# Nearest-neighbour upsampling: another order of the loads, and a first store of 56 rows

## The chip, the cores and the metric

The kernel runs on one core of one Trainium2 chip. The metric is device time of that core in microseconds (us), the median of several runs; lower is better. Beside the runs there is one profiled execution, from which all views of the trace come; its times count from the first instruction of the program.

## The reference

```python
def reference(x, scale_factor):                 # x: 16 x 64 x 64 x 64 float32, scale_factor 2
    ...
    for i in range(new_h):
        for j in range(new_w):
            src_i = i // scale_factor
            src_j = j // scale_factor
            result[:, :, i, j] = x[:, :, src_i, src_j].copy()
    return result.astype(np.float32)
```

Every input element becomes a block of 2 x 2 output elements. 16.78 MB come in, 67.11 MB go out, and nothing is calculated.

## The kernel before

**Tiling.** The input is a list of 65536 rows of 64 floats. It is cut into four quarters (`Q = 4`); in each quarter a partition holds 128 consecutive rows (`RQ`), so that all four quarters give a partition 512 rows. One input row of 64 floats becomes 256 output floats (two equal rows of 128), that is 1 KB of output a row.

**Memory.** One tile `mem` fills most of the on-chip memory: 79 output rows of free room (`WF`), and behind it the whole input (`xt`, 512 rows of 64 floats), the quarters in their natural order whatever the order of the loads.

**Loads (line 153).** Four DMAs, one for each quarter, issued by SyncE on its one queue. `begin_before_barrier` moves these four issues ahead of the opening barrier of the program.

**Groups (lines 162 to 177).** The 512 rows are worked off in order in ten groups, whose row counts stand in `rows` (line 141). For each group the rows are expanded within the on-chip memory (source: 64 floats a row, each read twice, the whole row twice; destination: one contiguous run), and then one DMA stores the group. Group 0 is copied by VectorE alone (line 171). Of the others VectorE copies `k * 9 // 32 * 2` rows, an even number, and ScalarE the rest (line 173). The store (line 176) is issued by SyncE on the same queue as the loads.

**Where the expanded rows lie.** Even groups start at offset 0 of `mem`, in the free room. Odd groups end just in front of the first input row that is not expanded yet, over input rows that are already used up. So group n + 2 takes room of group n and has to wait until store n has landed, and the copy of group n + 2 runs while store n + 1 is on the wire. Group 1 overwrites the input rows of group 0, so that its copies wait for the copy of group 0.

**Order.** All DMAs stand on one queue and are served in the order of their issue. SyncE waits before each store for the copies of its group. The waits follow from the overlaps in `mem`: a copy waits for the load of its input rows.

**End.** `close_early` rearranges the closing barrier so that only the wait for the last store stands at the end. The change does not touch it.

Of the kernel before, what the change touches and what calls it, by code (L numbers as in the profile page):

```python
# [1 line left out]

# [4 lines left out]

EARLY = 4  # L10


def begin_before_barrier(nc):

    blocks = nc.main_func.blocks
    main, body = blocks[0], blocks[1]
    sp = mybir.EngineType.SP
    loads = [i for i in body.instructions if i.engine == sp][:EARLY]  # L20
    for load in loads:
        assert isinstance(load, mybir.InstDMACopy), type(load)
        assert not (load.sync_info and load.sync_info.on_wait)
    names = [i.name for i in loads]
    body.instructions = [i for i in body.instructions if i.name not in names]
    kept = list(main.instructions)
    at = next(
        n
        for n, i in enumerate(kept)
        if i.engine == sp and isinstance(i, mybir.InstDrain)  # L30
    )
    kept[at:at] = loads
    main.instructions = kept


def close_early(nc):

    blocks = nc.main_func.blocks  # L40
    sp, pool = mybir.EngineType.SP, mybir.EngineType.Pool
    stores = [
        i
        for i in blocks[1].instructions
        if i.engine == sp and isinstance(i, mybir.InstDMACopy)
    ]
    last = stores[-1].sync_info.on_update[0].id

    end = list(blocks[-1].instructions)
    wait = end[0]  # L50
    assert wait.engine == sp and isinstance(wait, mybir.InstDrain)
    waits = list(wait.sync_info.on_wait)
    assert len({w.id for w in waits}) == len(waits) > 2
    assert all(w.wait_mode == "sem-ge-imm" for w in waits)

    mine = [i for i in end if i.engine == pool]
    kinds = [type(i).__name__ for i in mine]
    assert kinds == [
        "InstDrain",
        "InstEventSemaphore",  # L60
        "InstEventSemaphore",
        "InstDrain",
        "InstISA",
        "InstDrain",
        "InstEventSemaphore",
        "InstEventSemaphore",
    ], kinds
    d0, gather0, release0, d1, clear, d2, gather1, release1 = mine


    lo, hi = clear.ant_dict["range_first"], clear.ant_dict["range_last"]
    assert lo <= last <= hi and all(lo <= w.id <= hi for w in waits)
    clears = []
    for a, b in ((lo, last), (last + 1, hi + 1)):
        if a < b:
            clears.append(nc.gpsimd.sem_clear(range(a, b)).ins)

    landed = mybir.InstDrain(
        name=wait.name,
        engine=pool,  # L80
        debug=wait.debug,
        sync_info=mybir.SyncInfo(
            on_wait=[w for w in waits if w.id != last], on_update=[]
        ),
    )
    (w,) = [w for w in waits if w.id == last]
    final = mybir.InstEventSemaphore(
        name=clear.name,
        engine=sp,
        debug=wait.debug,  # L90
        sync_info=mybir.SyncInfo(
            on_wait=[w],
            on_update=[
                mybir.SyncUpdate(
                    sync_type=w.sync_type,
                    id=w.id,
                    ant_name=w.ant_name,
                    update_mode="sem-sub-imm",
                    update_value=w.wait_value,
                )  # L100
            ],
        ),
    )
    others = [i for i in end if i.engine != pool and i is not wait]
    blocks[-1].instructions = others + [
        d0, gather0, release0, gather1, release1, d1, landed, *clears, d2, final
    ]


@with_exitstack  # L110
def kernel(
    ctx: ExitStack,
    tc: tile.TileContext,
    x: bass.AP,
    scale_factor: int,
    out: bass.AP,
):
    nc = tc.nc
    nc.at_finalize(begin_before_barrier)
    nc.at_finalize(close_early)  # L120
    P = nc.NUM_PARTITIONS
    s = int(scale_factor)
    B, C, H, W = x.shape
    R = B * C * H // P
    fdt = x.dtype

    Q = 4
    RQ = R // Q  # L130
    xp = x.rearrange("b c h w -> (b c h) w").rearrange(
        "(q p r) w -> q p r w", q=Q, p=P
    )
    op = out.rearrange("b c (h hd) w -> (b c h) (hd w)", hd=s).rearrange(
        "(q p r) w -> q p r w", q=Q, p=P
    )

    rows = [63, 31, 34, 44, 42, 42, 64, 64, 64, 64]
    GROW = s * s
    FREE = 79
    WF = FREE * GROW * W
    assert sum(rows) == R
    mem_pool = ctx.enter_context(tc.tile_pool(name="mem", bufs=1))
    mem = mem_pool.tile([P, WF + R * W], fdt, name="mem")
    xt = mem[:, WF:].rearrange("p (r w) -> p r w", r=R)

    for q in range(Q):
        nc.sync.dma_start(out=xt[:, q * RQ : (q + 1) * RQ], in_=xp[q])

    def expanded(r0, r1):
        return (
            xt[:, r0:r1].unsqueeze(2).unsqueeze(4).to_broadcast([P, r1 - r0, s, W, s])
        )

    r0 = 0  # L160
    before = (0, 0)
    for n, k in enumerate(rows):
        size = k * GROW * W
        at = 0 if n % 2 == 0 else WF + r0 * W - size
        assert at >= before[1] or at + size <= before[0]
        before = (at, at + size)
        u = mem[:, at : at + size].rearrange(
            "p (k a w b) -> p k a w b", k=k, a=s, w=W
        )
        kv = k if n == 0 else k * 9 // 32 * 2  # L170
        nc.vector.tensor_copy(out=u[:, :kv], in_=expanded(r0, r0 + kv))  # L171
        if kv < k:
            nc.scalar.copy(out=u[:, kv:], in_=expanded(r0 + kv, r0 + k))  # L173
        q, f = divmod(r0, RQ)
        assert f + k <= RQ
        nc.sync.dma_start(out=op[q, :, f : f + k, :], in_=u)  # L176
        r0 += k


# [1 line left out]
_INS = ['x', 'scale_factor']  # L181
_OUTS = [((16, 64, 128, 128), 'float32')]

_NUMBERS = {'scale_factor': 2}


# [26 lines left out]
```

## Time and profile before

| | us |
|---|---|
| median of 3 runs (lowest, highest) | 198.25 (198.16, 198.26) |
| the profiled execution | 198.35 |
| its span, first to last instruction | 197.0 |
| VectorE busy, 10 copies | 51.2 |
| ScalarE busy, 9 copies and one table load | 46.3 |

Some words on reading the lines. DVE is VectorE, ACT is ScalarE, SP is SyncE, and a "q" behind a name means its sequencer. L171 is line 171. A group of instructions has its form (partitions x elements), its count, the busy time, the mean time of one in ns, and the idle time of its engine before it with what ended it. A timeline row has start and length in us. A row of windows has the stretch, its width, the busy time of DVE, ACT and POOL with counts, the granted clock, the DMA share and GB/s; share and GB/s count each packet whole in the window in which it starts, so that a narrow window can show more than 1.00. A DMA issue row has KB and the time from issue to landing.

### The profile page before, as it was taken

The numbers are of one execution on the slowest core, as the hardware profiler recorded it, in microseconds if no ns is written. First come the engines' busy times: TensorE is split into PE (matmuls) and PEld (weight loads), VectorE is DVE, ScalarE is ACT, GpSimd is POOL, SyncE is SP. The second block draws the span as 40 slices with busy tenths as digits, with TensorE's granted clock in tenths as the row PEclk, the third lists the DMA queues.
The fourth block names the chain that finished last, engine by engine and source line by source line (L and its number), as shares of the span: only waits on it lengthen the run. The fifth ranks groups of instructions, "written<-read, shape, count | busy, mean of one in ns | idle before, by whom it ended". The sixth has DMA issues, their size and how long they took to land.

```text
span 197.0 us, 107 instructions
## 1 busy us (share of the span) xinstructions
DVE 51.2 (26%) x10; ACT 46.3 (24%) x10; POOL 0.2 (0%) x4
## 2 busy tenths in 40 slices
DVE  0059993000005060510602706300720081000000
ACT  0020006000005262592002906500797000000000
POOL 0000000000000000000000000000000000000000
DMA  8999999999997999999999999999999999999994
GB/s 319 426 426 426 432 432 432 406 512 432 419 419 335 470 422 403 511 421 400 472 437 428 419 419 426 426 426 426 426 466 452 466 492 452 426 426 439 426 426 213
DMA packets 2016, 83.89 MB, mean 426 GB/s; under 512 B 224, under 2 KB 224, under 8 KB 224
## 3 DMA queue, kind: packets, MB, share of 16 engines
q1 hardware_dynamic: 2016, 83.89, 99.2%
HBM read 16.78 MB, written 67.11 MB: 426 GB/s over the span
## 4 chain that ended last, share of the span: by engine, by line
DMA 63%; DVE 13%; ACT 7%; issue 0%; DVEq 0%; ACTq 0%; SPq 0%
DMA out_dram<-mem 57%; DVE mem L171 13%; ACT mem L173 7%; DMA mem<-in_x_dram 6%; DVEq L171 0%; ACTq L173 0%; SPq L176 0%
## 5 line engine op out<-in xcount | busy, mean ns | idle before, releaser
L171 DVE COPY mem<-mem 128x9216 f32<-128x9216 f32 (+5 forms) x10 | 51.2, 5119 | 112.3 <-DMA out_dram<-mem 100.1
L173 ACT COPY mem<-mem 128x7168 f32<-128x7168 f32 (+3 forms) x9 | 45.0, 5005 | 92.9 <-DMA out_dram<-mem 77.2
L173 ACT ACT_TABLE_LOAD x1 | 1.3, 1283 | 12.2 <-DMA mem<-in_x_dram 12.2
L194 POOL MEMSET const-bfloat16-1.0<- 128x1 bf16 x1 | 0.1, 101 | 0.0
L194 POOL MEMSET const-uint8-127<- 128x1 uint8 x1 | 0.1, 101 | 0.0
L194 POOL MEMSET const-float32-0.0<- 128x1 f32 x1 | 0.1, 98 | 0.2 <-issue 0.2
L194 POOL MEMSET const-float32-1.0<- 128x1 f32 x1 | 0.1, 98 | 0.0
## 6 DMA issues: line engine op xcount, KB each, us to landing
mem<-in_x_dram SPq DMA_DIRECT2D x4, 4096.0 KB, 26.0
out_dram<-mem SPq DMA_DIRECT2D x2, 5376.0 KB, 21.8
out_dram<-mem SPq DMA_DIRECT2D x1, 8064.0 KB, 32.3
out_dram<-mem SPq DMA_DIRECT2D x1, 5632.0 KB, 19.0
out_dram<-mem SPq DMA_DIRECT2D x1, 4352.0 KB, 16.0
out_dram<-mem SPq DMA_DIRECT2D x1, 3968.0 KB, 38.2
out_dram<-mem SPq DMA_DIRECT2D x4, 32.4
```

The lines of the kernel that those rows point to most:

```text
L171: nc.vector.tensor_copy(out=u[:, :kv], in_=expanded(r0, r0 + kv))
L173: nc.scalar.copy(out=u[:, kv:], in_=expanded(r0 + kv, r0 + k))
L194: nc = _bacc.Bacc("TRN2", target_bir_lowering=False, num_devices=1)
```

## The change

The loads are issued in the order second, third, first, fourth quarter. They still go to the same places in `xt`, and the groups are still worked off from the first quarter on, so that group 0 now reads what the third load brings. The row counts of the first six groups change; each three still add up to 128. Group 0 is still copied by VectorE alone.

```diff
-    rows = [63, 31, 34, 44, 42, 42, 64, 64, 64, 64]
+    rows = [56, 36, 36, 48, 40, 40, 64, 64, 64, 64]
...
-    for q in range(Q):
+    for q in (1, 2, 0, 3):
         nc.sync.dma_start(out=xt[:, q * RQ : (q + 1) * RQ], in_=xp[q])
```

## The prediction

> **What bounds the kernel now.** I read the page first, then the waits, then short windows around the one place where the DMA queue turns from loads to stores.
>
> ```profile
> span 197.0 us, 107 instructions
> DVE 51.2 (26%) x10; ACT 46.3 (24%) x10; POOL 0.2 (0%) x4
> q1 hardware_dynamic: 2016, 83.89, 99.2%
> HBM read 16.78 MB, written 67.11 MB: 426 GB/s over the span
> ```
>
> The two copying engines work a quarter of the time each. The one DMA queue is occupied for 99.2% of 16 engines' span. So the kernel lasts as long as 83.89 MB take to move, and only what lies between transfers, or slows them, can be won or lost.
>
> ```profile
> DVE mem L171 <- DMA out_dram<-mem: 100.1, 8, 30.0
> ACT mem L173 <- DMA out_dram<-mem: 77.2, 6, 28.9
> 70.00:196.00 126.00, 29.38 (x7) 38.04 (x7) 0.00 (x0) 1.00 1.00 433
> ```
>
> The first two rows (waits) say that from the third copy on, the copying engines wait for stores to land and free their buffer, not the stores for them. The third row is a window: busy time of DVE, ACT and POOL, granted clock, DMA share, GB/s. From 70 to 196 us the queue has a share of 1.00 and moves 433 GB/s. Nothing is to be had there.
>
> The queue is served in order: load 1 to 4, then store 1, 2 and so on. A window as wide as the spread of the 16 engines holds one packet of each, so that share times width is the mean time of a packet: a window of 1.00 us shows it directly. A load packet is 32 KB (16 of them in 1.00 us show as 524 GB/s).
>
> ```profile
> 36.50:37.50 1.00, 0.00 (x0) 0.00 (x0) 0.00 (x0) 1.00 1.21 524
> 37.70:38.70 1.00, 0.00 (x0) 0.00 (x0) 0.00 (x0) 1.00 1.51 524
> 39.30:40.30 1.00, 0.00 (x0) 0.00 (x0) 0.00 (x0) 1.00 1.87 524
> 41.37:42.02 0.65, 0.00 (x0) 0.00 (x0) 0.00 (x0) 1.00 3.68 1588
> 43.70:44.70 1.00, 0.00 (x0) 0.00 (x0) 0.00 (x0) 1.00 2.38 1032
> ```
>
> A load packet takes 1.21 us, but the last two of load 4 on each engine take 1.51 and 1.87: 0.30 + 0.66 = 0.96 us lost on every engine. The fourth row is the first packet of store 1: 16 packets start between 41.37 and 42.02 and take 3.68 x 0.65 = 2.39 us, no more than the second (2.38). So the turn from reading to writing costs 0.96 us, and it is booked on the tail of the loads, not on the head of the stores.
>
> ```profile
> 0.89 0.43 SPq L153 DMA_DIRECT2D mem<-in_x_dram  x1
> mem<-in_x_dram SPq DMA_DIRECT2D x1, 4096.0 KB, 30.6
> 29.14 0.35 SPq L176 DMA_DIRECT2D out_dram<-mem  x1
> ```
>
> The third load is issued at 0.89 and lands 30.6 later, at 31.5. Store 1 is issued at 29.14, so it has been queued for over 8 us when those two slow packets begin. My reading: once an engine has read the last of load 4 it goes straight on to reading store 1 out of SBUF, while the end of load 4 is still being written into SBUF, and the two share a path.
>
> **The change, part by part.** *Order of the loads.* Four DMAs of 4096 KB on one queue, in another order: same bytes, same four issues ahead of everything else. The first quarter is now the third to land, so the first copy may not start before 31.5. The second and third quarter, which are first used by the fourth and seventh copy, land earlier than before; the fourth is last as before. Cost by itself: nothing.
>
> *First copy.* 56 rows of 256 output elements, 14336, on VectorE alone.
>
> ```profile
> 12.16 16.95 DVE L171 COPY mem<-mem 128x16128 f32<-128x16128 f32 x1 [12.16 <-DMA mem<-in_x_dram]
> 29.14 2.29 DVE L171 COPY mem<-mem 128x4096 f32<-128x4096 f32 x1
> L171 DVE COPY mem<-mem 128x4096 f32<-128x4096 f32 x1 | 2.3, 2294 | 0.0
> L171 DVE COPY mem<-mem 128x5632 f32<-128x5632 f32 x2 | 6.2, 3094 | 17.1 <-DMA out_dram<-mem 17.1
> L171 DVE COPY mem<-mem 128x9216 f32<-128x9216 f32 x4 | 19.8, 4960 | 46.0 <-DMA out_dram<-mem 46.0
> ```
>
> Two rates stand here. The copies of 4096 to 9216 elements lie on one line: (4960 - 2294) / 5120 = 0.521 ns an element and 161 ns fixed (5632 gives 3.094, measured 3.094). The first, of 16128, took 1.051 ns an element, twice as much. It differs in size, and in that its 63 rows are odd; every other VectorE part has an even row count by the code (16, 18, 24, 22, 22, 36). Transfers are not the reason: the 4096 one ran at the fast rate at 29.14, with loads still in flight. 14336 at the fast rate is 0.16 + 7.47 = 7.63 us, at the slow rate 15.07. By size it is nearer to the slow row; I take the fast one, since the fast rows show no bend up to 9216 and 56 is even. The Trainium skill ("VectorE: DVE Perf Modes", Mode 2×_2P) says that a one-source copy within SBUF gets two elements a cycle when the outermost dimension is even in source and destination, or odd and equal in both. Here the destination is one contiguous run and the source has 63 rows outermost, so by it 63 is slow and 56 fast; the trace agrees on all ten copies.
>
> So the first copy runs from 31.5 to 39.15 and store 1 is issued at 39.18 (before: the copy ended at 12.16 + 16.95 = 29.11, the issue came at 29.14). That is 10 us later than before, and the question is whether the queue notices.
>
> ```profile
> 0.00 1.89 SPq L153 DMA_DIRECT2D mem<-in_x_dram  x4
> 0.95:1.95 1.00, 0.00 (x0) 0.00 (x0) 0.00 (x0) 1.00 1.82 524
> 2.80:3.33 0.53, 0.00 (x0) 0.00 (x0) 0.00 (x0) 1.00 2.29 989
> 30.63:31.16 0.53, 0.53 (x1) 0.53 (x1) 0.00 (x0) 1.00 2.31 989
> ```
>
> *Would load 4 be over?* Its first packets start between 30.63 and 31.16 (last row: 2.31 x 0.53 = 1.21 us each). With no store behind it all eight would take 1.21, and it would end at 30.63 + 8 x 1.21 = 40.3 on the first engine and 40.85 on the last. So store 1 is issued 1.1 to 1.7 us before the engines run out.
>
> *How long from issue to stream?* The trace shows one start of an idle queue, load 1, issued at 0.00. All 16 first packets start 0.95 to 1.95 us after the issue and take 1.82 instead of 1.21; the second ones start at 2.80 to 3.33, which is as if a steady stream had begun 1.59 (first engine) to 2.12 us (last) after the issue. For store 1 that gives 39.18 + 1.59 = 40.77 to 39.18 + 2.12 = 41.30. Before, its packets began at 41.37 to 42.02. The stream of stores starts 0.60 to 0.72 us earlier, taken as 0.66: the 0.96 lost on the tail is saved, and some 0.3 us of it is given back in engines that wait for the late store. Bounds: at best the whole 0.96 is saved (store data come at once). At worst within this reading, the last first packet starts 1.95 after the issue and carries the full 0.61 extra: 39.18 + 1.95 + 0.61 = 41.74, a gain of 0.28. I keep 0.66, since it is the measured case of an idle queue.
>
> *The other row counts.* Bytes and number of stores stay the same, and the packet rate does not depend on their size (433 GB/s in the long window over all sizes). The pairs must still cover each other: copy n+2 runs while store n+1 is on the wire. The smallest store of the middle is now 36 rows, 4.7 MB, 10.9 us at 433 GB/s.
>
> ```profile
> L173 ACT COPY mem<-mem 128x7168 f32<-128x7168 f32 x4 | 24.7, 6167 | 36.8 <-DMA out_dram<-mem 36.7
> L173 ACT COPY mem<-mem 128x5120 f32<-128x5120 f32 x3 | 13.4, 4459 | 11.6 <-DMA out_dram<-mem 11.6
> L173 ACT COPY mem<-mem 128x4096 f32<-128x4096 f32 x1 | 3.6, 3607 | 28.9 <-DMA out_dram<-mem 28.9
> L173 ACT ACT_TABLE_LOAD x1 | 1.3, 1283 | 12.2 <-DMA mem<-in_x_dram 12.2
> ```
>
> ScalarE's part ends last. Of 36 rows it copies 16 (4096 elements, 3.61 us), of 48 it copies 22 (5632, about 4.9 between the rows for 5120 and 7168), of 64 it copies 28 (6.17). Add 2.1 to restart a queue: 7.0 against the 10.9 of a 36-row store, 8.3 against the 12.1 of a 40-row one. All hidden, with 3.8 us to spare at least; were that gone, each boundary would cost what is missing. Store 2 is issued at 39.18 + 3.61 = 42.8, behind 16.9 us of store 1 (7.34 MB at 433 GB/s). ScalarE's table load waits for the same load as before, now at 31.5; it ends 6 us before ScalarE's first copy. On SyncE nothing but the later stores is queued behind the longer wait.
>
> *Sum.* The profiled execution took 198.35 with its span of 197.0; less 0.66 is 197.69. The median of the runs is 198.25, 0.10 below, so 197.6.
>
> **The rivals.** *The turn is paid anyway.* The 0.96 could belong to the change of direction itself and not to the store queued behind the loads. For it: the trace has only this one turn. Against it: it sits on load packets, and the first store packet shows nothing. If the tail stays slow whatever is queued, the late store hides under it and nothing changes, 198.25; if it is paid after the restart, the last engine starts at 41.30 + 0.96 = 42.26 against 42.02, 198.5. Both are within what can be told from no change: I take 0.2%, 0.4 us, for that, throughout.
>
> *The queue runs dry (slower).* Place: between load 4 and store 1. No row shows a store put into an empty queue. It has to fetch from SBUF with nothing read ahead and then write to HBM; if that costs the turn and one more start of 0.61 us (1.82 - 1.21, seen for a load), the last engine starts at 41.30 + 0.96 + 0.61 = 42.87, 0.85 later than now: 199.1; half of the second part gives 198.8. It becomes a loss once issue to stream exceeds 42.02 - 39.18 = 2.84 us, and a loss of 0.4 at 3.24. Against it: the measured 2.12, and the first store packet of 2.39. The Trainium skill ("DMA: Bandwidth & Descriptors", Rules for kernel authors) speaks against this change: it advises to issue a DMA early, so that its fixed cost overlaps, and under Anatomy of one DMA puts that cost at about 2.0 us, for a DMA issued from GpSimd. By that figure, as an estimate, store 1 would begin at 39.18 + 2.0 = 41.2, hardly before today's first packet, and the gain would be 0.2 us; no row here shows which part of it falls ahead of the data.
>
> *The first copy is slow because it is large.* At 1.051 ns an element it takes 15.07, ends at 46.6, and the stream starts at 46.6 + 2.12 = 48.7, 6.7 us late: 205.0. It decides from a copy of 8.3 us on (7.63 + 0.72). For it: the one copy above 9216 elements is the slow one. Against it: the straight line of the others and the row counts.
>
> **How the numbers follow.** Chances: forecast 0.58, turn paid anyway 0.22, dry queue 0.15, slow copy 0.05. A little of the forecast (its worst bound, 198.0) counts as no change, 0.03, and some 0.01 of the dry queue does: faster 0.55, same 0.26, slower 0.19. Time 197.6. The range goes from 197.2 (0.96 saved is 197.3, and 0.1 for the spread of the runs) to 198.9, which takes in the turn and over half of the dry queue; the slow copy and the rest stay out. The forecast alone would have 197.2 to 198.0.
>
> **What would show it.** Load 4 now:
>
> ```profile
> 1.36 0.53 SPq L153 DMA_DIRECT2D mem<-in_x_dram  x1
> mem<-in_x_dram SPq DMA_DIRECT2D x1, 4096.0 KB, 41.0
> ```
>
> In the profile after: the first VectorE copy starts at 31.5 and takes 7.6 us; store 1 is issued near 39.2; the last two rounds of load 4 take close to 1.21 us, and load 4 lands over half a microsecond earlier than 1.36 + 41.0 = 42.4; the first packets of store 1 take longer than the second ones and the second ones start about 0.66 earlier than a shift by size alone would have it; a share of 1.00 from there to the end, and a span of 196.3. The prediction is wrong if the tail is as slow as before with the store not yet queued, if the first packets of store 1 end later than they did relative to their size, or if the copy takes 15 us.

## The result and the profile after

| | before | after |
|---|---|---|
| median of 21 runs, us | 198.26 | 197.93 |
| lowest to highest | 198.05 to 198.60 | 197.81 to 198.23 |
| span of the profiled execution | 197.0 | 196.7 |

The ratio of the two is 0.9983, with a 95% interval of 0.9976 to 0.9990: 0.33 us less, clear of zero, and half of the forecast 0.66. By the bound of 0.4 us that the prediction set, this counts as no change. The time lies within the range given, 197.2 to 198.9. The span is 196.7 where 196.3 was expected.

The page after, its lines on span, engines and queue:

```profile
span 196.7 us, 108 instructions
DVE 42.8 (22%) x10; ACT 46.1 (23%) x10; POOL 0.2 (0%) x4
q1 hardware_dynamic: 2016, 83.89, 99.1%
```

VectorE is busy 8.4 us less (the first copy runs at the fast rate now), and none of that shows in the time. A round, in what follows, is one packet on each of the 16 engines. Shown are the timeline of VectorE and SyncE, the two rows of load 4 (issue, then KB and time to landing), and windows of the kernel after: the second load round, the last load round, the first two store rounds and the last one. The last row is the last store round of the kernel before:

```profile
31.68 7.63 DVE L171 COPY mem<-mem 128x14336 f32<-128x14336 f32 x1 [31.68 <-DMA mem<-in_x_dram]
39.34 0.35 SPq L176 DMA_DIRECT2D out_dram<-mem  x1
1.36 0.53 SPq L153 DMA_DIRECT2D mem<-in_x_dram  x1
mem<-in_x_dram SPq DMA_DIRECT2D x1, 4096.0 KB, 40.0
...
2.99:3.43 0.44, 0.00 (x0) 0.00 (x0) 0.00 (x0) 1.00 2.76 1192
39.29:39.73 0.44, 0.44 (x2) 0.38 (x1) 0.00 (x0) 1.00 2.76 1192
40.59:41.09 0.50, 0.50 (x1) 0.50 (x1) 0.00 (x0) 1.00 4.32 1835
42.74:43.24 0.50, 0.00 (x0) 0.21 (x1) 0.00 (x0) 1.00 4.28 1835
193.32:193.87 0.55, 0.00 (x0) 0.00 (x0) 0.00 (x0) 1.00 4.40 1907
...
193.59:194.24 0.65, 0.00 (x0) 0.00 (x0) 0.00 (x0) 1.00 3.72 1613
```

Share times width is again the mean packet. The last round of load 4 takes 2.76 x 0.44 = 1.21 us: the slow tail is gone, and load 4 lands at 1.36 + 40.0 = 41.4 instead of 42.4. Now follow the engine that is last in each round, by the right edge of its window; it need not be the same engine in every round. From the second load packet to the first store packet it took 42.02 - 3.33 = 38.69 before. After the change load 4 ends at 39.73 + 1.21 = 40.94, which is 37.51 after 3.43: 1.18 saved. The first store packet then starts at 41.09, 0.15 later. From the first store packet to the last one it took 194.24 - 42.02 = 152.22 before, and 193.87 - 41.09 = 152.78 after: 0.56 lost, spread over 153 us in which the queue does not run empty (a share of 1.00 from 120 to 190 us). With 0.10 by which this execution began its stream later (3.43 against 3.33), the sum is -1.18 + 0.15 + 0.56 + 0.10 = -0.37, and the last packets start 0.37 earlier.

So the change won more than was thought at the turn, and gave 0.7 of it back, most of it in a place where nothing had been expected: the stores themselves run 0.4% slower to the end.

### The profile page after: what moved, and what is told of

Its sections match the earlier page's. It is cut to its first block, busy times and chain, and to the rows that moved or that the text cites. A ratio compares the mean times of both kernels' runs of the same rounds, so it can differ in the third digit from the quotient of the medians.

```text
span 196.7 us, 108 instructions
## 1 busy us (share of the span) xinstructions
DVE 42.8 (22%) x10; ACT 46.1 (23%) x10; POOL 0.2 (0%) x4
## 4 chain that ended last, share of the span: by engine, by line
DMA 67%; DVE 8%; ACT 7%; SPq 0%; issue 0%; DVEq 0%; ACTq 0%
DMA out_dram<-mem 51%; DMA mem<-in_x_dram 16%; DVE mem L171 8%; ACT mem L173 7%; SPq L153 0%; DVEq L171 0%; ACTq L173 0%; SPq L176 0%
## 5 line engine op out<-in xcount | busy, mean ns | idle before, releaser
L171 DVE COPY mem<-mem 128x9216 f32<-128x9216 f32 (+4 forms) x10 | 42.8, 4293 | 120.1 <-DMA out_dram<-mem 88.5
L173 ACT ACT_TABLE_LOAD x1 | 1.3, 1283 | 31.7 <-DMA mem<-in_x_dram 31.7
```

## The experiments

What was open: is it the time of the issue that removes the slow tail, or the order of the loads; do the stores run slower because of the issue too, or because of the new row counts; and what does a really empty queue cost? "Bare pace" below is that of the kernel before, 152.2 us from the first to the last store packet of the last engine; this time is called the stretch. The sum of bytes in it is the same in every kernel. The ratio of an experiment is to runs of the kernel before that were taken beside it.

### Natural order of the loads

```diff
-    for q in (1, 2, 0, 3):
+    for q in range(Q):
```

> The new row counts, the loads in their natural order: the first copy can start at 12.2, takes 7.6, and store 1 is issued near 19.9, long before the loads end. Theory A (reading ahead): a store that is queued when an engine has read its last load packet is read ahead; that slows the tail of the loads by about 1 us, and fills a reserve that lets every later store packet run at its bare pace. So the last two load rounds take about 1.5 and 1.9 us instead of 1.21, the 64-row packets take 2.418 us with no scatter, the stretch from the last load packet to the last store packet is 154.6 us, and the time is that of the kernel before, 198.25 (ratio 1.000). Theory B (the row counts make the store packets slow, the late issue saves the tail): slow tail and slow packets (2.422), stretch 155.2, time 198.8.

198.34, ratio 1.0002 (0.9990 to 1.0013). Issue row, the last two load rounds, the first and the last store round:

```profile
19.91 0.35 SPq L176 DMA_DIRECT2D out_dram<-mem  x1
...
37.86:38.50 0.64, 0.00 (x0) 0.00 (x0) 0.00 (x0) 1.00 2.04 819
39.29:39.71 0.42, 0.00 (x0) 0.00 (x0) 0.00 (x0) 1.00 4.82 1248
41.21:41.78 0.57, 0.00 (x0) 0.00 (x0) 0.00 (x0) 1.00 3.73 1610
193.42:193.99 0.57, 0.00 (x0) 0.00 (x0) 0.00 (x0) 1.00 4.24 1840
```

The load rounds take 1.31 and 2.02 us: 0.9 lost, as before the change. The stretch is 193.99 - 41.78 = 152.21, the bare pace, with the new row counts. Theory B falls: the row counts make nothing slow.

### Store 1 issued earlier, with loads and rows of the changed kernel

```diff
-        kv = k if n == 0 else k * 9 // 32 * 2
+        kv = 40 if n == 0 else k * 9 // 32 * 2     # and 48, 44, 52, 50 in the other runs
```

ScalarE copies the rest of group 0 beside VectorE, so that the copy ends earlier. Loads, rows and stores stay as they are. ScalarE now starts at 31.8 instead of 39.3, and its table load runs at 2.3 instead of 31.7.

> The changed kernel, but of group 0 VectorE copies 40 rows and ScalarE 16, side by side, so that store 1 is issued near 37.2 instead of 39.34, with loads and rows as in the changed kernel. Theory A: its first packets are queued 1 to 2 us later, at 38.2 to 39.2, which is before the engines have read all of load 4 (by the tail of the kernel before, up to about 1 us ahead of its end at 40.5): slow tail again, bare pace after it, time 198.25. Theory C (the order of the loads, not the time of the issue, takes the slow tail away): tail at 1.21, store packets as in the changed kernel, time 197.9.

> As the run before with 48 rows for VectorE and 8 for ScalarE: store 1 is issued near 38.3, its packets queued at 39.3 to 40.3, when the engines are reading the last of load 4. Theory A: reading ahead for some engines and in part: a tail that costs 0.2 to 0.7 us, store packets between the two paces, time between 197.6 and 198.2. Theory C: as the changed kernel, 197.9, tail at 1.21.

40 rows: 198.13, ratio 0.9998 (0.9989 to 1.0007). 48 rows: 197.27, ratio 0.9954 (0.9942 to 0.9967). The rows of the first (issue, the last two load rounds, first and last store round):

```profile
37.37 0.35 SPq L176 DMA_DIRECT2D out_dram<-mem  x1
...
37.97:38.65 0.68, 0.68 (x1) 0.68 (x1) 0.00 (x0) 1.00 2.20 771
39.46:40.18 0.72, 0.55 (x1) 0.72 (x1) 0.00 (x0) 1.00 2.48 728
41.25:42.08 0.83, 0.00 (x0) 0.00 (x0) 0.00 (x0) 1.00 2.56 1105
193.48:194.29 0.81, 0.00 (x0) 0.00 (x0) 0.00 (x0) 1.00 2.99 1295
```

Rounds of 1.50 and 1.79, 0.86 lost, and a stretch of 152.21: the tail is as slow as before, with the second, third, first and fourth quarter in the changed order. Theory C falls: the order of the loads does not take the slow tail away; it only sets the time of the issue. The 48-row kernel was a surprise. Theory A, that bare pace is paid for with the tail, had it between 197.6 and 198.2. It came out 0.9 us below the kernel before. It was run a second time:

> The kernel that issued store 1 near 38.3 (48 rows of group 0 on VectorE, 8 on ScalarE) once more, to see whether its ratio of 0.9954 holds: 197.3, tail at 1.21 to 1.25, store packets at the bare pace. If the earlier result was chance in where the 16 engines stood, 197.6 to 197.9.

197.31, ratio 0.9945 (0.9933 to 0.9958). Issue, last load round, first and last store round of this second run:

```profile
38.36 0.35 SPq L176 DMA_DIRECT2D out_dram<-mem  x1
...
39.00:39.78 0.78, 0.78 (x1) 0.78 (x1) 0.00 (x0) 1.00 1.56 672
40.21:40.99 0.78, 0.78 (x1) 0.78 (x1) 0.00 (x0) 1.00 2.72 1176
192.65:193.21 0.56, 0.00 (x0) 0.00 (x0) 0.00 (x0) 1.00 4.32 1872
```

The last load round takes 1.56 x 0.78 = 1.22, the first store round 2.72 x 0.78 = 2.12 (2.16 in the changed kernel), and the stretch is 193.21 - 40.99 = 152.22. No slow tail and the bare pace together: the whole gain of the turn with nothing given back. This is the fastest version found; its interval does not touch that of the changed kernel. Three more issue times show where it ends on both sides:

> The changed kernel with 44 of the 56 rows of group 0 on VectorE and 12 on ScalarE, so that store 1 is issued near 37.8, between the runs that issued it at 37.4 (tail slow by 0.9 us, bare pace) and 38.3 (tail not slow, bare pace). Theory A' (what the time of the issue decides: the earlier the store is queued ahead of the end of the loads, the more it slows their tail, up to about 1 us; queued too late, the engines finish reading the loads first and the store packets never reach the bare pace): the cost of the tail falls off in between, about half, time 197.7. A threshold instead of a slope would give 197.3 or 198.2.

> 50 rows on VectorE, 6 on ScalarE: store 1 issued near 38.55, between 38.3 (197.27) and 38.8 (197.68, scattered from 197.34 to 198.06). Theory A' with engines that go late one by one: some engines at the bare pace, some not, 197.3 to 197.7.

> As the run before with 52 rows on VectorE and 4 on ScalarE: store 1 is issued near 38.8, between 38.3 (ratio 0.9954) and 39.34 (0.9983). Theory A': no slow tail; bare pace as long as the packets are queued before the engines have read the last load; 197.3 if 0.5 us later is still in time, 197.9 if not.

44 rows: 197.67, ratio 0.9971 (0.9960 to 0.9981). 50 rows: 197.35, ratio 0.9949 (0.9935 to 0.9963). 52 rows: 197.68, ratio 0.9963 (0.9950 to 0.9977). In the same order, for each the issue, then the last load round (44 rows alone; in the other two it takes 1.21) and the first and the last store round:

```profile
37.71 0.35 SPq L176 DMA_DIRECT2D out_dram<-mem  x1
...
39.21:39.67 0.46, 0.46 (x1) 0.46 (x1) 0.00 (x0) 1.00 3.51 1140
40.76:41.32 0.56, 0.00 (x0) 0.56 (x1) 0.00 (x0) 1.00 3.80 1639
192.98:193.55 0.57, 0.00 (x0) 0.00 (x0) 0.00 (x0) 1.00 4.24 1840
```

```profile
38.74 0.35 SPq L176 DMA_DIRECT2D out_dram<-mem  x1
...
40.34:41.12 0.78, 0.78 (x1) 0.78 (x1) 0.00 (x0) 1.00 2.74 1176
192.77:193.58 0.81, 0.00 (x0) 0.00 (x0) 0.00 (x0) 1.00 2.99 1295
```

```profile
38.83 0.35 SPq L176 DMA_DIRECT2D out_dram<-mem  x1
...
40.33:40.90 0.57, 0.57 (x1) 0.57 (x1) 0.00 (x0) 1.00 3.77 1610
192.54:193.69 1.15, 0.00 (x0) 0.00 (x0) 0.00 (x0) 1.00 2.10 912
```

At 37.71 the tail loses 3.51 x 0.46 - 1.21 = 0.40 and the stretch is 152.23. At 38.74 it is 152.46 (this profiled execution, 197.69, was the slowest of its runs) and at 38.83 152.79. Both sides are slopes, and the valley lies between 38.3 and 38.7 (197.27, 197.31 and 197.35). A' had asked for a slope on the early side and left the late side open. On the late side the engines go late one by one, as the expectation for 50 rows had it: at 38.83 the first edges of the two store rounds are 192.54 - 40.33 = 152.21 apart, so at least one engine keeps the bare pace, while the last edges are 152.79 apart. At 39.34 the first edges show the loss too (193.32 - 40.59 = 152.73).

### The old row counts, issued late

```diff
-    for q in range(Q):
+    for q in (1, 0, 2, 3):      # in the kernel before
```

> The kernel before with its own row counts, only the first two loads exchanged (second, first, third, fourth): group 0 can start at 21.9, its 63 rows take 16.95 at the slow rate, and store 1 is issued near 38.9. Theory A': the time of the issue alone decides, so tail at 1.21, and 197.3 to 197.9 like the runs issued at 38.8 to 39.3. If the new row counts are needed for the gain: 198.2.

197.78, ratio 0.9976 (0.9966 to 0.9987).

```profile
38.95 0.35 SPq L176 DMA_DIRECT2D out_dram<-mem  x1
...
39.02:39.68 0.66, 0.66 (x1) 0.66 (x1) 0.00 (x0) 1.00 1.84 794
40.28:40.90 0.62, 0.62 (x1) 0.62 (x1) 0.00 (x0) 1.00 3.90 1665
192.77:193.65 0.88, 0.00 (x0) 0.00 (x0) 0.00 (x0) 1.00 2.75 1192
```

The old rows, their first copy still at the slow rate, and yet the gain of the change: tail at 1.84 x 0.66 = 1.21, stretch 152.75. What counts here is when store 1 is issued, not which rows it has nor how fast they were copied.

### Store 1 issued into an empty queue

```diff
         nc.vector.tensor_copy(out=u[:, :kv], in_=expanded(r0, r0 + kv))
+        if n == 0:
+            nc.vector.tensor_copy(out=u[:, :20], in_=expanded(r0, r0 + 20))
```

> The changed kernel with 20 rows of group 0 copied a second time by VectorE, so that store 1 is issued 2.8 us later, near 42.15, with the queue empty since 40.5 to 40.9. If a store starts from an empty queue as load 1 did, its stream begins 1.6 to 2.1 us after the issue, 43.7 to 44.3 instead of 40.6 to 41.1 in the changed kernel: time 201.1. If it starts as quickly as it seems to in the changed kernel (at most 1.2 us from issue to first packet and 0.04 us extra on it), 200.4. The dry-queue rival of the prediction (the turn of 0.96 and one more start paid after the restart): 202 and more. Theory A also wants store packets as slow as in the changed kernel (2.422), with no reserve.

202.74, ratio 1.0228 (1.0214 to 1.0242). The issue came later than planned, at 44.90 and not 42.15, since the extra copy was put behind VectorE's part of group 1. Issue, last load round, first two and last store rounds:

```profile
44.90 0.35 SPq L178 DMA_DIRECT2D out_dram<-mem  x1
...
39.11:39.83 0.72, 0.72 (x2) 0.00 (x0) 0.00 (x0) 1.00 1.68 728
45.74:45.90 0.16, 0.00 (x0) 0.16 (x1) 0.00 (x0) 1.00 13.46 5734
47.89:48.05 0.16, 0.00 (x0) 0.16 (x1) 0.00 (x0) 1.00 13.34 5734
198.48:198.68 0.20, 0.00 (x0) 0.00 (x0) 0.00 (x0) 1.00 12.11 5243
```

The times of the expectation don't hold for this issue, but the start can be read: first packets 0.84 to 1.00 us after the issue, and 13.46 x 0.16 = 2.15 us long, 0.04 over the bare 2.12. No turn is paid at the start. The stretch is 198.68 - 45.90 = 152.78, that of the changed kernel. So the dry-queue rival is refuted in its price, and the lasting slowness of the stores does not grow with the time that the queue was empty: an issue at 39.34, before the end of the loads, costs as much of it as one 4 us after their end.

### A copy within HBM between the loads and the stores

```diff
         nc.sync.dma_start(out=xt[:, q * RQ : (q + 1) * RQ], in_=xp[q])
+    spare = nc.dram_tensor("spare", [P, 32, W], fdt).ap()
+    nc.sync.dma_start(out=spare, in_=xp[0, :, :32])      # in the kernel before
```

> The kernel before with one more DMA on the queue, issued after load 4 and ahead of store 1: it copies 1 MB of the input to a spare place in HBM and touches no SBUF. The output does not use it. It adds 2.4 us or more of queue time. Theory P (the tail is slow because store data are read out of SBUF while load data are written into it): with this copy behind load 4 the last load rounds take 1.21. Theory Q (anything that is queued behind the loads slows their tail): 1.5 and 1.9 again.

200.74, ratio 1.0122 (1.0106 to 1.0137). Last load round, the start of the copy, a later part of it, the first store round (with six packets of the copy in the window) and the last one:

```profile
39.08:39.65 0.57, 0.00 (x0) 0.00 (x0) 0.00 (x0) 1.00 2.13 920
40.29:40.62 0.33, 0.00 (x0) 0.00 (x0) 0.00 (x0) 1.00 0.48 199
42.00:42.70 0.70, 0.00 (x0) 0.00 (x0) 0.00 (x0) 1.00 1.16 304
43.67:44.21 0.54, 0.00 (x0) 0.00 (x0) 0.00 (x0) 1.00 4.64 2003
195.89:196.42 0.53, 0.00 (x0) 0.00 (x0) 0.00 (x0) 1.00 4.56 1978
```

The last load round takes 2.13 x 0.57 = 1.21, so theory Q falls: not anything that is queued behind slows the loads. The copy also writes to HBM, so a write to HBM behind the loads does not slow them by itself. But the loss may not be gone. Packets of the copy are 8 KB; 199 GB/s x 0.33 us are 8 of them, at 0.48 x 0.33 x 16 / 8 = 0.32 us each. An engine has 8 of them, which is 2.5 us, so on the last engine the copy should end at 39.65 + 1.21 + 2.5 = 43.4. Its first store packet starts at 44.21, 0.8 later. The later row shows it: 304 GB/s x 0.70 us are 26 packets, at 1.16 x 0.70 x 16 / 26 = 0.50 us each. The copy writes nothing into SBUF. So theory P has its 1.21, but its reason is in doubt: if the 0.8 is the loss of the tail, then what stands directly ahead of the stores is slowed whether it writes to SBUF or not. That is argued and not shown, since no run has the copy without stores queued behind it, and its first packets may not be its lasting pace. The stretch is 196.42 - 44.21 = 152.21.

### An even first group of 64 rows

```diff
-    rows = [63, 31, 34, 44, 42, 42, 64, 64, 64, 64]
+    rows = [64, 30, 34, 44, 42, 42, 64, 64, 64, 64]      # in the kernel before
```

> The kernel before with 64 and 30 instead of 63 and 31 rows in the first two groups: an even count that is larger than the 63 of the slow copy. If an odd count makes the copy slow, 16384 elements take 0.16 + 8.53 = 8.7 us, and store 1 is issued near 20.9; if the size does, 17.2 and 29.4. Theory A' in both cases: issued early, slow tail, bare pace, 198.2.

198.27, ratio 0.9998 (0.9989 to 1.0007). The group of this copy:

```profile
L171 DVE COPY mem<-mem 128x16384 f32<-128x16384 f32 x1 | 8.7, 8694 | 12.3 <-DMA mem<-in_x_dram 12.3
20.97 0.35 SPq L176 DMA_DIRECT2D out_dram<-mem  x1
```

One row more than 63, and half the time: 8.69 against 16.95 us. The odd count makes this copy slow, not its size. The time does not move, since the store is early either way.

## Why the prediction was right, and where not

**Right.** The mechanism of the turn, as far as the time of the issue goes. The first copy started at 31.68 (31.5 was said) and took 7.63 (7.63), at the fast rate; store 1 was issued at 39.34 (39.18); the last load rounds took 1.21; the table load, the other row counts and the pairs of copy and store cost nothing; the sign was right, and the place of the gain. That the tail is slow because of a store queued early was shown by moving the issue with loads, rows and stores unchanged: 0.86 lost at 37.37, 0.40 at 37.71, nothing at 38.36.

**Mis-sized: the tail.** 0.96 was the mean over the engines. For the engine that is last in each round the turn was worth 1.18.

**Mis-sized the other way: from issue to stream.** The start of load 1 was taken as the measure, 1.59 to 2.12 us with 0.61 on the first packet. A store from an empty queue took 0.84 to 1.00 and 0.04. By these 0.84 to 1.00 its packets would have been in place at 40.2 to 40.3 in the changed kernel, before load 4 ended at 40.5 to 40.9; even so 0.15 was lost there, against the 0.3 that was allowed.

**Failed: the bare pace of the stores.** The step "the packet rate does not depend on their size" held for sizes, but the prediction took from it that the stores would run as before to the end. Issued at 39.34, they took 0.56 longer over the whole way; that is what halves the forecast. A share of 1.00 was named as its sign, and windows of 1.00 and 433 GB/s cannot show 0.4%: the difference of two narrow windows, 150 us apart, does.

**Luck.** The two sizes at the turn came out better than forecast, by 0.22 and 0.15 us, and the pace of the stores came out worse, by 0.56. With the pace alone missed, 0.10 would have been left of the 0.66. That so much of the forecast came true is in part two misses going against a third.

**The rivals.** The turn paid anyway fell: the tail went. The dry queue fell in its price: no turn, 0.04 on the first packet; what a late issue does cost, the 0.56 on the way, was in no rival. The slow large copy fell with the copy of 64 rows. The Trainium skill's advice to issue early ("DMA: Bandwidth & Descriptors", Rules for kernel authors) is half of the truth here: issued 0.5 us too late the store loses, but issued early it costs 0.9 us against the best time.

**The reason that was given** for the slow tail, reading store data out of SBUF while load data are written into it, was not shown. The copy within HBM speaks against it, but does not settle it, since the copy's own pace without a store behind it is not known. What the runs leave standing is that a first store that is queued early enough slows the loads directly ahead of it, and that a copy within HBM in the place of the store does not. What is shared was not found. The copying engines' own use of SBUF is not the cause: in the kernel before both stood idle during the two slow rounds (the prediction's rows from 37.70 and 39.30), and at 38.36 both worked all through the last load round (0.78 of 0.78 us), which was fast. Nor was it shown why stores that were queued too late stay slower to the end. A reserve of data read ahead, which an early queue fills and a late one never gets, would fit; but a reserve bought with the tail does not explain the issue at 38.36, which has the pace and did not pay.

## What to carry to other kernels

In a kernel that lasts as long as its DMA queue, the time at which a transfer joins the queue matters even while the queue is full: here the first store was best issued 1.9 to 2.6 us before the engines ended the loads (38.36 against 40.2 to 41.0), which is 0.8 us of 198 below an issue 1 us earlier and 0.6 below one 1 us later. Move such an issue alone, in steps of half a microsecond, and look at both sides of the turn, the packets ahead of it and the pace behind it. To say that nothing else changes needs a view that can resolve the change: times of the same packet far apart, not a share.

## What was not expected of the hardware

- The stretch of the stores, for the engine that ends last, is 152.21 to 152.23 us for every issue up to 38.36 and 152.75 to 152.79 from 38.83 on, with 152.46 at 38.74; in between the engines go late one by one. The loss is then spread over the way, somewhat more of it early. The rows below are the first round of the first 64-row store, in the changed kernel and in the natural order of the loads. Up to it, from the first store round, the two took 118.81 - 41.09 = 77.72 and 119.14 - 41.78 = 77.36. From it to the last store round they took 193.87 - 118.81 = 75.06 and 193.99 - 119.14 = 74.85. So 0.36 was lost in the first half and 0.21 in the second.

```profile
118.30:118.81 0.51, 0.00 (x0) 0.00 (x0) 0.00 (x0) 1.00 4.77 2056
118.57:119.14 0.57, 0.00 (x0) 0.00 (x0) 0.00 (x0) 1.00 4.26 1840
```

- A store into an empty queue had its first packets 0.84 to 1.00 us after the issue, where load 1 at the start of the program had them after 0.95 to 1.95.
- A copy within HBM that was put between the loads and the stores kept the tail of the loads at its 1.21 us; the copy itself ended 0.8 us later than its first packets promised.
